# Gates, branch projections and merge of a hybrid decoder layer: features on the partitions against tokens on the partitions

## The chip, the core and the metric

The kernel runs on one core of a Trainium2 chip. The time is the device time of one execution in microseconds (us), the median of three. The core has five engines that this document names by the profile's short names: PE multiplies matrices (its weight loads are listed apart, as PEld), DVE and ACT work element by element on up to 128 partitions, POOL does the same more slowly, and SP issues the loads from HBM. Each engine takes its instructions in order and waits on semaphores that the others raise.

## The reference

One layer on 256 tokens of width 1024. The input, normalised, is multiplied by one wide matrix; its columns give the queries, keys, values and gates of two branches and two merge gates. Each branch ends in a gated activation of 256 x 1024, which has its own output projection. The change lies in the last lines:

```python
ret = jnp.einsum('bsv,vd->bsd', ret, w_ret_o)
mo = merge_heads(mo) * jax.nn.silu(mg)
mo = jnp.einsum('bsv,vd->bsd', mo, w_moba_o)
y = jax.nn.sigmoid(gr) * ret + jax.nn.sigmoid(gm) * mo
return x + jnp.einsum('bsd,de->bse', y, w_out)
```

A final RMSNorm follows.

## The kernel before, in words

All weights are streamed through the chip once, in 24 groups of 512 columns. A group comes as four chunks of two K tiles (a K tile is 128 of the 1024 rows). ACT rounds each chunk to a high part `wh` (L108) and DVE subtracts it from the raw chunk to get the low part `wl` (L109); both have eight buffers, so two groups fit. The loop splits group g + 1 and loads group g + 2 while PE multiplies group g. Products with at least 256 moving columns are made three times over, high by high, high by low and low by high, and accumulated in PSUM.

A group is multiplied in one of two layouts, both with the same 49,152 columns of PE work in a group:

- N, `proj_n` (L195 to L197): tokens on the partitions. The activations are the stationary operand, the weights move, 512 columns at a time. For each of two token tiles there are 8 K tiles of three products: 24 products.
- T, `proj_t` (L210, L211): features on the partitions. The weights are stationary, the activations move. For each of four feature tiles there are 8 K tiles of two products, one of 512 columns (high and low part of the activations side by side) and one of 256.

A unit is half a group: one token tile of N, or two feature tiles of T. Units run in order, u = 2 * group + half, and pieces of attention and small transposes are set ahead of some of them. The tile framework's scheduler orders each engine's instructions by the order of the code and the buffers that come free.

Groups 14 to 17 are the merge gates, 18 and 19 the retention branch's output projection, 20 and 21 that of the other branch, 22 and 23 the last projection. Before the change 14 to 21 are T, and the last projection is N. A T unit's PSUM is emptied for each feature tile in `evac_t`: ACT copies one half (L370), DVE adds the other (L371), and then comes a factor (L372): the token's 1/rms for gates, the gate itself for a branch. For groups 20 and 21 DVE adds the two branches (L407), ACT rounds the sum (L408) and DVE takes the low part (L409); that is `yT`, features on the partitions, which the last projection takes as its stationary operand as it is.

The retention branch's gated output is turned by PE in four sets of four 128 x 128 transposes (`ret_transpose`, L351) into a PSUM tile with one buffer, tag `t`. The last projection ends with the norm of each token tile and the stores.

Of the kernel before, what the change touches and what calls it, by code (L numbers as in the profile page):

```python
"""Hybrid decoder layer (RMSNorm, retention branch, MoBA branch, gated merge, residual, final RMSNorm)
for 256 tokens of width 1024 on one core.

Layouts: a tensor is "N" with tokens on the partitions and "T" with features on the partitions.
Each projection is either N (activations stationary, weights moving, 512 columns) or T (weights
stationary, activations moving, 256 tokens), so that the consumer finds the layout that it needs.

Products with at least 256 moving columns run in float32r (12-bit significands, one pass each): every
operand a is split exactly into a = ah + al with ah = round12(a), al = a - ah, and ah*bh + ah*bl + al*bh are
accumulated in float32. Attention products with 128 moving columns are plain float32 matmuls.  # L10

With 256 tokens the MoBA branch has a single block of 256, so no query has a past block: the top-k
selection is empty for any input, and each query attends causally to its own block.
"""
# [34 lines left out]
def hybrid_kernel(ctx: ExitStack, tc, xT, x, w_in, gn_w, w_ret_o, w_moba_o, w_out, fn_w, decay, out):  # L49
# [10 lines left out]
    def win(c):  # L60
# [8 lines left out]
        (win(GR), "T"), (win(GR + GW), "T"), (win(GM), "T"), (win(GM + GW), "T"),  # L69
        (w_ret_o[:, 0:GW], "T"), (w_ret_o[:, GW:], "T"),  # L70
        (w_moba_o[:, 0:GW], "T"), (w_moba_o[:, GW:], "T"),
# [19 lines left out]
    def cut(g, k):  # L91
        """Column ranges in which K tile k of group g is handled."""
        return (slice(0, S), slice(S, GW)) if (g, k) == (0, 0) else (slice(0, GW),)
# [24 lines left out]
    # K tile 0 of group 0 comes in two column ranges: its banks are started by products of zeros.  # L118
# [18 lines left out]
    # rel[q, k] = k - q for the causal pairs, MASKED for the others; query tile 0 with keys 0..127,  # L137
    # query tile 1 with keys 0..255.
# [16 lines left out]
    def rsqrt(y, a, tmp):  # L155
        """y = a ** -0.5 (a is kept): square root, exact reciprocal, one Newton step."""
        nc.scalar.activation(tmp, a, AF.Sqrt)
        nc.vector.reciprocal(y, tmp)
        nc.vector.tensor_mul(tmp, y, y)
        nc.vector.tensor_mul(tmp, tmp, a)  # L160
        nc.vector.tensor_scalar(tmp, tmp, -0.5, 1.5, op0=ALU.mult, op1=ALU.add)
        nc.vector.tensor_mul(y, y, tmp)
# [5 lines left out]
    def x_stats():  # L168
        """1 / rms per token: per partition for N, along the free axis for T."""
        ss = cst.tile([P, NT], F32, name="ss")  # L170
        tmp = cst.tile([P, NT], F32, name="sst")
        for t in range(NT):
            nc.scalar.activation(reto[:, t], xn[:, t], AF.Square, accum_out=ss[:, t:t + 1])
        nc.vector.tensor_scalar(ss, ss, 1.0 / D, EPS, op0=ALU.mult, op1=ALU.add)
        rsqrt(rs, ss, tmp)
# [10 lines left out]
    def proj_n(g, ah, al, t, c0=0, n=GW, ps=None):  # L186
        """[128 tokens of tile t, n columns of the group from c0], added to ps if that is given."""
        begun = ps is not None
        if not begun:
            ps = pm.tile([P, GW], F32, name="ps_m", tag="m")[:, :n]  # L190
        sl = slice(t * P, (t + 1) * P)
        for k in range(KT):
            for cs in cut(g, k) if g == 0 else (slice(0, n),):
                h, l = (w[g, k // 2][:, k % 2, c0 + cs.start:c0 + cs.stop] for w in (wh, wl))
                nc.tensor.matmul(ps[:, cs], ah[:, k, sl], h, start=not begun and k == 0, stop=False)  # L195
                nc.tensor.matmul(ps[:, cs], ah[:, k, sl], l, start=False, stop=False)  # L196
                nc.tensor.matmul(ps[:, cs], al[:, k, sl], h, start=False, stop=k == KT - 1)  # L197
        return ps

    def proj_t(g, a, i):  # L200
        """Feature tile i of the group: [128 features, 2, 256 tokens], the two halves still to be added.

        a(k) holds the high and the low part side by side, so that the high part of the weights meets both
        in one product of 512 columns.
        """
# [9 lines left out]
    qT, kT, V = {}, {}, {}  # L215
    # High and low parts of what the scores take in float32r: of the retention all queries and the first
    # 128 keys, of MoBA the last 128 queries and all keys.
# [126 lines left out]
    def ret_transpose(i):  # L344
        """Feature tiles 2i, 2i + 1 of the gated retention output, split."""
# [14 lines left out]
    G = {}  # L360
    mT = []
    yTh = yTl = None
    A = None

    def evac_t(g, i, ps):
        """Feature tile i of group g: adds the two halves of ps and applies what follows."""
        f = (i + 4) if g in (7, 8, 13, 15, 17, 19, 21) else i

        def scaled(out, w, eng=nc.gpsimd):
            nc.scalar.activation(out, ps[:, 1], AF.Copy)  # L370
            nc.vector.tensor_add(out, ps[:, 0], out)  # L371
            eng.tensor_mul(out, out, w)  # L372
# [22 lines left out]
        elif g in (14, 15, 16, 17):  # L395
            z = tmp("z")
            scaled(z, rsb)
            if i % 2 == 0:
                gt = new_v("gt")
                G[g // 16, f], G[g // 16, f + 1] = gt[:, :S], gt[:, S:]  # L400
            nc.scalar.activation(G[g // 16, f], z, AF.Sigmoid)  # L401
        elif g in (18, 19):
            scaled(A[:, f], G[0, f])
        elif g in (20, 21):
            z = tmp("z")
            scaled(z, G[1, f], nc.vector)
            nc.vector.tensor_add(z, z, A[:, f])  # L407
            nc.scalar.activation(yTh[:, f], z, AF.Copy)  # L408
            nc.vector.tensor_sub(yTl[:, f], z, yTh[:, f].bitcast(F32))  # L409

    def evac_n(g, t, ps):
# [17 lines left out]
        elif g in (10, 11):  # L429
            nc.scalar.activation(rgate[:, t, (g - 10) * GW:(g - 9) * GW], ps, AF.Copy, scale=r1)  # L430

# [8 lines left out]
    def unit(g, i):  # L440
        """Half i of group g: a token tile (N) or two feature tiles (T)."""
        nonlocal A, yTh, yTl, rgate
        if i == 0:
# [14 lines left out]
            if g == 18:  # L458
                A = ac.tile([P, KT, S], F32, name="A", tag="rgate")
            if g == 20:  # L460
                yT = ac.tile([P, 2, KT, S], F32R, name="yT", tag="xs")
                yTh, yTl = yT[:, 0], yT[:, 1]
        if groups[g][1] == "N":
            evac_n(g, i, proj_n(g, xh, xl, i, ps=ps0[i] if g == 0 else None))
        else:
            if g < 18:
                a = lambda k: xs[:, k]
            elif g < 20:
                a = lambda k: rT[k // 2][:, k % 2]
            else:  # L470
                a = lambda k: mT[k // 4][:, k % 4]
# [20 lines left out]
    # Unit u = 2 * group + half: the attention pieces come before the projection unit that they are set at.  # L492
# [15 lines left out]
    at(37, moba_split)  # L508

    nc.gpsimd.dma_start(gnw, gn_w)  # L510
    fnw = None
    for g in range(NG - 2):
        for i in range(2):
            u = 2 * g + i
            for c in (2 * i, 2 * i + 1):
                split(g + 1, c)
                if g + 2 < NG:
                    load(g + 2, c)
# [5 lines left out]
            if u == 38:  # L524
                # The last columns of x, split: TensorE adds them to the last product.
# [5 lines left out]
            if u == 40:  # L531
                fnw = ac.tile([P, D], F32, name="fnw", tag="qk", bufs=4)
                nc.sync.dma_start(fnw, fn_w.to_broadcast([P, D]))
                nc.gpsimd.tensor_scalar_mul(fnw, fnw, 2.0)
            for f, a in extra.get(u, []):
                f(*a)
            unit(g, i)
    for c in range(4):
        split(NG - 1, c)

    # Output projection, residual and final norm, one token tile after the other. Of the last columns
    # only what needs them is left for the end.
    r = ac.tile([P, NT, D], F32, name="r", tag="oT")
    sc = cst.tile([P, NT, 5], F32, name="sc")
    for t in range(NT):
        part, a, s, y, v = (sc[:, t, j:j + 1] for j in range(5))
        pieces = ((0, 512), (512, 1024)) if t == 0 else ((0, 512), (512, 768), (768, 1024))
        for j, (c0, c1) in enumerate(pieces):
# [4 lines left out]
            if c1 - c0 == S and last:  # L553
# [3 lines left out]
                proj_n(22 + c0 // GW, yTh, yTl, t, c0 % GW, c1 - c0, ps)  # L557
                nc.scalar.activation(sq, ps, AF.Square, accum_out=ss)
                nc.vector.tensor_mul(rr, ps, ww)
            else:  # L560
                ps = proj_n(22 + c0 // GW, yTh, yTl, t, c0 % GW, c1 - c0)
# [10 lines left out]
        # One Newton step from s, about sqrt(a): sqrt(a) = (s + a / s) / 2; the 2 is in fnw.  # L572
# [14 lines left out]
def _decay_table(np):  # L587
    """decay[m, h, :]: gamma_h ** (n - m) / sqrt(dk) for key m of tile 0 with queries n of 0..255, then for
    key m of tile 1 with the queries of tile 1; 0 where n < m."""
# [37 lines left out]
```

## Time and profile before

| | us |
|---|---|
| median of three runs (305.37 to 306.14) | 305.88 |
| span of the profiled execution, first to last instruction | 303.3 |
| PE busy in it | 294.0 |
| DVE, ACT, POOL busy in it | 219.7, 186.7, 79.0 |

The profile is of one execution; its span leaves out about 2.6 us around it. A matmul's row in the timeline has a start and a modelled end, and rows overlap, so what a product costs in a dense stretch is the distance from start to start.

### The profile page before, as it was taken

What the parts mean: (1) busy time and instruction counts of PE and PEld (TensorE: products, weight loads), DVE (VectorE), ACT (ScalarE), POOL (GpSimd) and SP (SyncE); (2) the same over time, 40 slices, a digit from 0 to 9 for tenths busy, and PEclk for the clock granted to TensorE, in tenths of its full rate; (3) what the DMA queues carried; (4) which work ended last, traced back from release to release, by engine and by line L of the source; (5) the groups of instructions that cost most, each with busy time, mean ns of one, the idle gap of its engine ahead of it and who ended that gap; (6) DMA issues with size and microseconds to landing.
All of it is one profiled execution on the core that took longest, in us unless ns stands there. A gap on an engine that the chain in (4) does not pass through costs nothing.

```text
span 303.3 us, 4584 instructions
## 1 busy us (share of the span) xinstructions
PE 294.0 (97%) x1628; PEld 253.9 (84%) x1628; DVE 219.7 (72%) x374; ACT 186.7 (62%) x358; POOL 79.0 (26%) x92
## 2 busy tenths in 40 slices
PE   8999989899999999999999999999999999999992
PEld 5778878799988899888888888888888888888891
DVE  3868676868699694884746799685784788899342
ACT  5786655755748676675966657476575556646231
POOL 3000185564520346300000132432432442300000
PEclk9999999999999999999999999999999999999998
DMA  7999967646384552746166264754835759540021
GB/s 188 361 405 407 319 166 244 212 161 193 91 254 108 189 181 100 195 143 218 36 240 200 79 163 123 216 166 168 261 93 201 253 177 304 169 140 0 0 73 69
DMA packets 28969, 55.11 MB, mean 182 GB/s; under 512 B 1937, under 2 KB 3985, under 8 KB 28945
## 3 DMA queue, kind: packets, MB, share of 16 engines
q1 hardware_dynamic: 28624, 54.54, 55.6%
q8 instruction: 13, 0.21, 0.3%
q10 hardware_dynamic: 288, 0.26, 0.3%
q14 instruction: 12, 0.09, 0.1%
q0 software_dynamic: 32, 0.00, 0.0%
HBM read 53.75 MB, written 1.05 MB: 181 GB/s over the span
## 4 chain that ended last, share of the span: by engine, by line
PE 89%; DVE 3%; POOL 3%; ACT 1%; issue 1%; DVEq 0%; ACTq 0%
PE ps_m L210 34%; PE ps_m L211 18%; PE ps_m L196 10%; PE ps_m L195 10%; PE ps_m L197 10%; DVE wl L109 2%; POOL qT L372 2%; POOL rqs L239 1%; PE ps_s L117 1%; PE ps_t L265 1%; ACT wh L108 1%; PE ps_s L244 1%; PE ps_o L284 1%; PE ps_t L351 1%; PE ps_o L316 1%
## 5 line engine op out<-in xcount | busy, mean ns | idle before, releaser
L210 PE MATMUL ps_m<-xs,wh 128*128 128x512 f32 x384 | 134.7, 393 | 0.0
L109 DVE TENSOR_TENSOR wl<-raw,wh 128x1024 fp32r<-128x1024 f32 x88 | 115.4, 1331 | 17.2 <-ACT wh L108 16.8
L211 PE MATMUL ps_m<-xs,wl 128*128 128x256 f32 x384 | 108.1, 282 | 1.1 <-DVE wl L109 1.1
L108 ACT ACTIVATE wh<-raw 128x1024 fp32r<-128x1024 f32 x88 | 90.1, 1052 | 4.4 <-PE ps_m L197 2.0
L210 PEld LDWEIGHTS ps_m<-xs,wh 128*128 128x128 f32 x384 | 72.1, 188 | 14.6
L211 PEld LDWEIGHTS ps_m<-xs,wl 128*128 128x128 f32 x384 | 72.7, 189 | 1.6 <-DVE wl L109 1.4
L372 POOL TENSOR_TENSOR z<-z,rsb 128x256 f32<-128x256 f32 x24 | 23.8, 990 | 88.4 <-DVE z L371 88.4
L196 PE MATMUL ps_m<-wl,xs 128*128 128x512 f32 (+1 forms) x98 | 38.9, 398 | 0.0
L197 PE MATMUL ps_m<-wh,xs 128*128 128x512 f32 (+1 forms) x98 | 38.8, 396 | 0.0
L195 PE MATMUL ps_m<-wh,xs 128*128 128x512 f32 (+1 forms) x98 | 38.7, 403 | 0.0
L196 PEld LDWEIGHTS ps_m<-wl,xs 128*128 128x128 f32 x98 | 19.0, 193 | 4.9 <-DVE wl L106 1.1
L195 PEld LDWEIGHTS ps_m<-wh,xs 128*128 128x128 f32 x98 | 18.9, 194 | 4.4 <-ACT wh L105 0.7
L197 PEld LDWEIGHTS ps_m<-wh,xs 128*128 128x128 f32 x98 | 18.9, 193 | 3.9
L210 PE MATMUL ps_m<-rT,wh 128*128 128x512 f32 x64 | 22.2, 390 | 0.0
L210 PE MATMUL ps_m<-mT,wh 128*128 128x512 f32 x64 | 22.2, 390 | 0.0
L371 DVE TENSOR_TENSOR z<-ps_m,z 128x256 f32<-128x256 f32 x32 | 13.4, 418 | 7.5 <-ACT z L370 7.5
L211 PE MATMUL ps_m<-rT,wl 128*128 128x256 f32 x64 | 18.1, 282 | 0.0
L211 PE MATMUL ps_m<-mT,wl 128*128 128x256 f32 x64 | 18.1, 282 | 0.0
L401 ACT ACTIVATE gt<-z 128x256 f32<-128x256 f32 x16 | 6.7, 418 | 16.8 <-POOL z L372 16.8
L210 PEld LDWEIGHTS ps_m<-rT,wh 128*128 128x128 f32 x64 | 12.0, 188 | 2.5
L210 PEld LDWEIGHTS ps_m<-mT,wh 128*128 128x128 f32 x64 | 12.0, 188 | 2.5
L195 PE MATMUL ps_m<-wh,yT 128*128 128x512 f32 (+1 forms) x40 | 14.0, 350 | 0.0
(171 smaller groups left out, 424.7 us busy)
## 6 DMA issues: line engine op xcount, KB each, us to landing
raw<-in_w_in SPq DMA_DIRECT2D x68, 512.0 KB, 4.7
raw<-in_w_ret_o SPq DMA_DIRECT2D x8, 512.0 KB, 5.1
raw<-in_w_moba_o SPq DMA_DIRECT2D x8, 512.0 KB, 5.0
raw<-in_w_out SPq DMA_DIRECT2D x8, 512.0 KB, 5.7
raw<-in_w_in SPq DMA_DIRECT2D x7, 256.0 KB, 4.5
xn<-in_x SPq DMA_DIRECT2D x2, 512.0 KB, 8.1
xt<-in_xT SPq DMA_DIRECT2D x7, 128.0 KB, 4.5
dec<-in_decay SPq DMA_DIRECT2D x1, 768.0 KB, 10.7
```

The lines of the kernel that those rows point to most:

```text
L108: nc.scalar.activation(h, r, AF.Copy)
L109: nc.vector.tensor_sub(l, r, h.bitcast(F32))
L117: nc.tensor.matmul(pw, warm[:, :P], warm, start=True, stop=True)
L195: nc.tensor.matmul(ps[:, cs], ah[:, k, sl], h, start=not begun and k == 0, stop=False)
L196: nc.tensor.matmul(ps[:, cs], ah[:, k, sl], l, start=False, stop=False)
L197: nc.tensor.matmul(ps[:, cs], al[:, k, sl], h, start=False, stop=k == KT - 1)
L210: nc.tensor.matmul(ps, h, a(k), start=k == 0, stop=False)
L211: nc.tensor.matmul(ps[:, 0], l, a(k)[:, 0], start=False, stop=k == KT - 1)
L239: nc.gpsimd.tensor_sub(out[:, 1], a, out[:, 0].bitcast(F32))
L371: nc.vector.tensor_add(out, ps[:, 0], out)
L372: eng.tensor_mul(out, out, w)
L401: nc.scalar.activation(G[g // 16, f], z, AF.Sigmoid)
```

## The change

Groups 14 to 21 become N. The merge gates are one ACT sigmoid of 128 x 512 straight from PSUM, with the token's 1/rms as a scale per partition. A branch's projection is multiplied by its gate on DVE, 128 x 512 at a time. The merged rows are then tokens on the partitions, but the last projection needs them with features there: `merge_transpose(t, c)` turns four 128 x 128 tiles on PE into one PSUM tile of tag `t`, ACT rounds it to the high part of `yT` and DVE takes the low part. It is called four times. The units of groups 20 and 21 now run 20.0, 21.0, 20.1, 21.1, so that token tile 0 is complete two units before token tile 1, and the splits of groups 22 and 23 move with them. The split of the other branch's output (`moba_split`) and the residual's last columns (`xr`) are set two units earlier.

```diff
-        (win(GR), "T"), (win(GR + GW), "T"), (win(GM), "T"), (win(GM + GW), "T"),
-        (w_ret_o[:, 0:GW], "T"), (w_ret_o[:, GW:], "T"),
-        (w_moba_o[:, 0:GW], "T"), (w_moba_o[:, GW:], "T"),
+        (win(GR), "N"), (win(GR + GW), "N"), (win(GM), "N"), (win(GM + GW), "N"),
+        (w_ret_o[:, 0:GW], "N"), (w_ret_o[:, GW:], "N"),
+        (w_moba_o[:, 0:GW], "N"), (w_moba_o[:, GW:], "N"),
...
-        elif g in (14, 15, 16, 17):
-            z = tmp("z")
-            scaled(z, rsb)
-            if i % 2 == 0:
-                gt = new_v("gt")
-                G[g // 16, f], G[g // 16, f + 1] = gt[:, :S], gt[:, S:]
-            nc.scalar.activation(G[g // 16, f], z, AF.Sigmoid)
-        elif g in (18, 19):
-            scaled(A[:, f], G[0, f])
-        elif g in (20, 21):
-            z = tmp("z")
-            scaled(z, G[1, f], nc.vector)
-            nc.vector.tensor_add(z, z, A[:, f])
-            nc.scalar.activation(yTh[:, f], z, AF.Copy)
-            nc.vector.tensor_sub(yTl[:, f], z, yTh[:, f].bitcast(F32))
...
+        elif g in (14, 15, 16, 17):
+            G[g // 16, t, g % 2] = gt = new_v("gt")
+            nc.scalar.activation(gt, ps, AF.Sigmoid, scale=r1)
+        elif g in (18, 19):
+            nc.vector.tensor_mul(A[:, t, (g - 18) * GW:(g - 17) * GW], ps, G[0, t, g % 2])
+        elif g in (20, 21):
+            z, y = G[1, t, g % 2], A[:, t, (g - 20) * GW:(g - 19) * GW]
+            nc.vector.tensor_mul(z, ps, z)
+            nc.vector.tensor_add(y, y, z)
+
+    def merge_transpose(t, c):
+
+        ps = pa.tile([P, 4, P], F32, name="ps_t", tag="t", bufs=1)
+        for j in range(4):
+            k = 4 * c + j
+            nc.tensor.transpose(ps[:, j], A[:, t, k * P:(k + 1) * P], ident)
+        h, l = (yT[:, 4 * c:4 * c + 4, j, t * P:(t + 1) * P] for j in range(2))
+        nc.scalar.activation(h, ps, AF.Copy)
+        nc.vector.tensor_sub(l, ps, h.bitcast(F32))
...
-    for g in range(NG - 2):
+    for g in range(NG - 4):
...
+    for i in range(2):
+        stream(20, i)
+    yT = ac.tile([P, KT, 2, S], F32R, name="yT", tag="xs")
+    unit(20, 0)
+    unit(21, 0)
+    unit(20, 1)
+    for c in range(2):
+        merge_transpose(0, c)
+    for i in range(2):
+        stream(21, i)
+    unit(21, 1)
...
+            if t == 0:
+                merge_transpose(1, j)
```

The order of the built program shows where the scheduler puts the new pieces. On PE, before, the last product of group 21 (`mT` is the other branch's output, `ps_m` a projection's PSUM) is followed at once by the last projection:

```order
L210 MATMUL ps_m<-mT_2568,wh 128x512
L211 MATMUL ps_m<-mT_2568,wl 128x256
L195 MATMUL ps_m<-wh,yT 128x512
L196 MATMUL ps_m<-wl,yT 128x512
L197 MATMUL ps_m<-wh,yT 128x512
```

On PE, of the change, the same place: the last product of unit 20.1, the first set of merge transposes and the start of unit 21.1; then the second set, after 16 of the 24 products of 21.1; then the first product of the last projection. (The names of tokens' merged rows are `A`, of the transposes' PSUM `ps_t`.)

```order
L197 MATMUL ps_m<-wh,mT_2332 128x512
L431 MATMUL ps_t<-ident,A 128x128 x4
L195 MATMUL ps_m<-wh,mT_2331 128x512
...
L195 MATMUL ps_m<-wh,mT_2332 128x512
L431 MATMUL ps_t<-ident,A 128x128 x4
L196 MATMUL ps_m<-wl,mT_2332 128x512
...
L195 MATMUL ps_m<-wh,yT 128x512
```

The sets are split apart: the second stands not behind the first but inside the next unit.

On DVE, of the change, the merge of token tile 0 (L423, L424 twice), the splits of group 22 (L109), the product of unit 20.1, the last split of group 22, its sum, and the low part of the first set (L434), which has to be done before the second set may overwrite `ps_t`:

```order
L423 TENSOR_TENSOR gt<-ps_m,gt 128x512
L424 TENSOR_TENSOR A<-A,gt 128x512
L109 TENSOR_TENSOR wl<-raw,wh 128x1024 x3
L423 TENSOR_TENSOR gt<-ps_m,gt 128x512
L109 TENSOR_TENSOR wl<-raw,wh 128x1024
L424 TENSOR_TENSOR A<-A,gt 128x512
L434 TENSOR_TENSOR yT<-ps_t,yT 128x4x128
L106 TENSOR_TENSOR wl<-raw,wh 128x512 x3
L434 TENSOR_TENSOR yT<-ps_t,yT 128x4x128
```

A whole split and a sum stand between the product of 20.1 and the first low part.

On ACT, of the change, there: the splits of groups 20, 21 and 22 in a row, and then the high parts of the sets (L433) between those of group 23 (L105):

```order
L108 ACTIVATE wh<-raw 128x1024 x12
L433 ACTIVATE yT<-ps_t 128x4x128
L105 ACTIVATE wh<-raw 128x512 x4
L433 ACTIVATE yT<-ps_t 128x4x128
```

The first high part stands behind the last split of group 22.

## Rows read from the trace of the kernel before

**Rows 1.** The page: span, busy time, slices, chain that ended last.

```profile
span 303.3 us, 4584 instructions
...
PE 294.0 (97%) x1628; PEld 253.9 (84%) x1628; DVE 219.7 (72%) x374; ACT 186.7 (62%) x358; POOL 79.0 (26%) x92
...
PE   8999989899999999999999999999999999999992
...
POOL 3000185564520346300000132432432442300000
PEclk9999999999999999999999999999999999999998
...
PE 89%; DVE 3%; POOL 3%; ACT 1%; issue 1%; DVEq 0%; ACTq 0%
```

**Rows 2.** What PE waited for in the span: total, times, longest.

```profile
PE ps_s L117 <- DVE warm L114: 1.2, 1, 1.2
PE ps_o L316 <- DVE il L303: 1.1, 1, 1.1
PE ps_m L211 <- DVE wl L109: 1.1, 1, 1.1
```

**Rows 3.** PE in four stretches: length, busy (instructions), clock, DMA share, GB/s.

```profile
122.25:127.85 5.60, 5.60 (x27) 1.00 0.76 200
213.42:274.53 61.11, 61.11 (x355) 1.00 0.59 196
274.53:291.33 16.80, 16.80 (x75) 1.00 0.02 8
178.42:189.97 11.55, 11.55 (x70) 1.00 0.54 147
```

**Rows 4.** Timeline of PE around transposes: start us, length us, instruction, count.

```profile
189.85 0.28 PE L211 MATMUL ps_m<-xs,wl 128*128 128x256 f32 x1
189.97 0.60 PE L351 MATMUL ps_t<-ident,reto 128*128 128x128 f32 x4
190.33 0.48 PE L210 MATMUL ps_m<-xs,wh 128*128 128x512 f32 x1
```

**Rows 5.** Groups of PE instructions: busy us, mean ns, idle before.

```profile
L351 PE MATMUL ps_t<-ident,reto 128*128 128x128 f32 x16 | 2.4, 273 | 0.0
```

**Rows 6.** Groups of POOL, ACT and DVE that the change removes in part.

```profile
L372 POOL TENSOR_TENSOR z<-z,rsb 128x256 f32<-128x256 f32 x24 | 23.8, 990 | 88.4 <-DVE z L371 88.4
...
L401 ACT ACTIVATE gt<-z 128x256 f32<-128x256 f32 x16 | 6.7, 418 | 16.8 <-POOL z L372 16.8
...
L371 DVE TENSOR_TENSOR z<-ps_m,z 128x256 f32<-128x256 f32 x32 | 13.4, 418 | 7.5 <-ACT z L370 7.5
```

**Rows 7.** Groups of ACT and DVE: splits, and 128x512 from PSUM.

```profile
L108 ACT ACTIVATE wh<-raw 128x1024 fp32r<-128x1024 f32 x88 | 90.1, 1052 | 4.4 <-PE ps_m L197 2.0 <-DMA raw<-in_w_in 1.5 <-PE ps_m L210 0.6
...
L430 ACT ACTIVATE rgate<-ps_m,rs 128x512 f32<-128x512 f32 x4 | 2.7, 682 | 6.3 <-PE ps_m L197 6.2
...
L109 DVE TENSOR_TENSOR wl<-raw,wh 128x1024 fp32r<-128x1024 f32 x88 | 115.4, 1331 | 17.2 <-ACT wh L108 16.8 <-PE ps_o L283 0.2
...
L562 DVE TENSOR_TENSOR r<-ps_m,xn 128x512 f32<-128x512 f32 x3 | 2.1, 692 | 4.5 <-PE ps_m L197 4.5
```

**Rows 8.** Timeline of DVE: two single splits.

```profile
193.45 1.76 DVE L109 TENSOR_TENSOR wl<-raw,wh 128x1024 fp32r<-128x1024 f32 x1
...
266.08 1.22 DVE L109 TENSOR_TENSOR wl<-raw,wh 128x1024 fp32r<-128x1024 f32 x1
```

**Rows 9.** Timeline of all engines at the end.

```profile
296.65 0.28 PE L196 MATMUL ps_m<-wl,yT 128*128 128x256 f32 x1
...
296.76 0.28 PE L197 MATMUL ps_m<-wh,yT 128*128 128x256 f32 x1
...
297.12 0.28 PE L197 MATMUL ps_m<-wh,yT 128*128 128x256 f32 x1
297.49 0.38 ACT L558 ACTIVATE sq<-ps_m 128x256 f32<-128x256 f32 x1 [2.15 <-PE ps_m L197]
```

More of the change, by code (lines that the diff above doesn't have):

```diff
@@ L183, in x_stats_t, with proj_n @@
         nc.scalar.activation(rsq, ps[:, :S], AF.Copy, scale=1.0 / math.sqrt(P))
-    def proj_n(g, ah, al, t, c0=0, n=GW, ps=None):
+    def proj_n(g, a, t, c0=0, n=GW, ps=None):
         begun = ps is not None
@@ L194, in proj_n @@
                 h, l = (w[g, k // 2][:, k % 2, c0 + cs.start:c0 + cs.stop] for w in (wh, wl))
-                nc.tensor.matmul(ps[:, cs], ah[:, k, sl], h, start=not begun and k == 0, stop=False)
-                nc.tensor.matmul(ps[:, cs], ah[:, k, sl], l, start=False, stop=False)
-                nc.tensor.matmul(ps[:, cs], al[:, k, sl], h, start=False, stop=k == KT - 1)
+                nc.tensor.matmul(ps[:, cs], a(k)[:, 0, sl], h, start=not begun and k == 0, stop=False)
+                nc.tensor.matmul(ps[:, cs], a(k)[:, 0, sl], l, start=False, stop=False)
+                nc.tensor.matmul(ps[:, cs], a(k)[:, 1, sl], h, start=False, stop=k == KT - 1)
         return ps
@@ L361, in hybrid_kernel, with scaled @@
     mT = []
-    yTh = yTl = None
+    yT = None
     A = None
     def evac_t(g, i, ps):
-        f = (i + 4) if g in (7, 8, 13, 15, 17, 19, 21) else i
-        def scaled(out, w, eng=nc.gpsimd):
+        f = (i + 4) if g in (7, 8, 13) else i
+        def scaled(out, w):
             nc.scalar.activation(out, ps[:, 1], AF.Copy)
             nc.vector.tensor_add(out, ps[:, 0], out)
-            eng.tensor_mul(out, out, w)
+            nc.gpsimd.tensor_mul(out, out, w)
         def tmp(n):
@@ L440, in unit @@
     def unit(g, i):
-        nonlocal A, yTh, yTl, rgate
+        nonlocal A, yT, rgate
         if i == 0:
@@ L458, in unit @@
             if g == 18:
[L459 to L462, printed above, removed]
+                A = ac.tile([P, NT, D], F32, name="A", tag="rgate")
+        if g < 18:
+            a = lambda k: xs[:, k]
+        elif g < 20:
+            a = lambda k: rT[k // 2][:, k % 2]
+        else:
+            a = lambda k: mT[k // 4][:, k % 4]
         if groups[g][1] == "N":
-            evac_n(g, i, proj_n(g, xh, xl, i, ps=ps0[i] if g == 0 else None))
+            evac_n(g, i, proj_n(g, a, i, ps=ps0[i] if g == 0 else None))
         else:
[L466 to L471, printed above, removed]
             for f in (2 * i, 2 * i + 1):
@@ L507, in hybrid_kernel, with stream @@
         at(27 + 2 * i, ret_transpose, i)
-    at(37, moba_split)
+    at(35, moba_split)
     nc.gpsimd.dma_start(gnw, gn_w)
-    fnw = None
-    for g in range(NG - 2):
+    def stream(g, i):
+        for c in (2 * i, 2 * i + 1):
+            split(g + 1, c)
+            if g + 2 < NG:
+                load(g + 2, c)
+    for g in range(NG - 4):
         for i in range(2):
             u = 2 * g + i
[L515 to L518, printed above, removed]
+            stream(g, i)
             if u == 0:
@@ L523, in hybrid_kernel @@
                 x_stats_t()
-            if u == 38:
+            if u == 36:
                 xr = new_v("xr", F32R)
@@ L530, in hybrid_kernel @@
                 nc.vector.tensor_sub(xr[:, S:], xn[:, 1, D - S:], xr[:, :S].bitcast(F32))
[L531 to L534, printed above, removed]
             for f, a in extra.get(u, []):
@@ L537, in hybrid_kernel, with ya @@
             unit(g, i)
+    fnw = ac.tile([P, D], F32, name="fnw", tag="qk", bufs=4)
+    nc.sync.dma_start(fnw, fn_w.to_broadcast([P, D]))
+    nc.gpsimd.tensor_scalar_mul(fnw, fnw, 2.0)
+    for i in range(2):
[9 more added lines that the diff above has]
+    unit(21, 1)
     for c in range(4):
         split(NG - 1, c)
+    def ya(k):
+        return yT[:, k]
     r = ac.tile([P, NT, D], F32, name="r", tag="oT")
@@ L556, in hybrid_kernel @@
                 nc.tensor.matmul(ps, ir, xr[:, S:], start=False, stop=False)
-                proj_n(22 + c0 // GW, yTh, yTl, t, c0 % GW, c1 - c0, ps)
+                proj_n(22 + c0 // GW, ya, t, c0 % GW, c1 - c0, ps)
                 nc.scalar.activation(sq, ps, AF.Square, accum_out=ss)
@@ L560, in hybrid_kernel @@
             else:
-                ps = proj_n(22 + c0 // GW, yTh, yTl, t, c0 % GW, c1 - c0)
+                ps = proj_n(22 + c0 // GW, ya, t, c0 % GW, c1 - c0)
                 nc.vector.tensor_add(rr, ps, xn[:, t, c0:c1])
```

## The prediction

> **What bounds the kernel now.** The page comes first: PE is busy for 294.0 of 303.3 us, its slices read 8 or 9 but for the last, its granted clock reads 9 throughout, the upper of its two levels (2.4 GHz); the chain that ended last is PE for 89% [rows 1]. Busy time of PE is made of overlapping rows, so the second view is PE's own waits: three in the whole span, 3.4 us together [rows 2]. The first is the start, the other two wait for DVE at 43.7 and 60.3 us, long before the change begins (its first unit, 28, stands one unit before the transposes at 189.97, near 184 us). So from 60 us on PE waits for nothing, and a change behind that point is worth what it adds to or takes from PE's own instructions, plus any wait that it makes. Work taken from DVE, ACT and POOL earns nothing.
>
> The third view is therefore PE's length for a unit. Eleven T units from 213.42 to 274.53 take 61.11 us, 5.555 each; all of them belong to groups that change. The first three N units of the last projection take 16.80, 5.600 each, and a lone N unit among attention pieces takes 5.60 as well [rows 3]. The fourth is what four transposes cost between projection products: they start at 189.97 and the next product at 190.33 [rows 4].
>
> **The change part by part.** *T to N.* Eight groups are 16 units. Each goes from 5.555 to 5.600: 16 x 0.045 = +0.7 us. From below: if an N product ran at T's time per column, the unit would be 5.555 too and the term 0. From above: without the one slow resumption after transposes (0.08) in the window, T is 5.548, and the term 0.8. I take 0.7, since the N row is the very form that is added.
>
> A rule on this stands in the Trainium skill, "TensorE: Matmul & The Clock Gate", section "Back-to-back issue gap": each matmul costs its columns plus a fixed 2.5 ns, so fewer and longer ones should win. By its figures, as an estimate, the 24 products of N would take 5.18 us and the 32 of T 5.20, and the term would be -0.3 instead of +0.7. The trace does not agree: both units are longer than that, and N is the longer one [rows 3]. The sum goes by the rows.
>
> *Transposes.* There are 16 more, in four sets of four, of the kind and number of the retention's sets, again between float32r products. The stretch from one set to the next holds a set and two T units: 11.55 - 2 x 5.555 = 0.44 us for a set [rows 3], 0.36 of it the set itself [rows 4] and the rest, 0.08, a slower first product behind it. Four sets: +1.8 us. From below 0.36 a set, 1.4; from above one after the other at 273 ns each, 16 x 0.273 = 4.4 [rows 5]. I take 1.8, the row that is the same operation in the same place. Before, the merge needed none of this, since `yT` came out of the sum in the right layout, beside PE.
>
> *What goes off the other engines.* POOL loses 16 of the 24 multiplies of the z row (0.99 us each) and eight of A, ACT 16 sigmoids of 0.42, 32 copies and eight roundings, DVE 32 adds of 0.42, 24 of them in the z row, and 24 operations of the merge [rows 6]; in their place stand eight sigmoids and four roundings on ACT and 16 operations on DVE, of 128 x 512 and some 0.7 us [rows 7]. All of it lay beside PE, which had no wait there, so I cost it at nothing. The freed time has no taker either.
>
> *Weights.* An N group asks for its chunks over its first 5.6 us, a T group for all four inside its first feature tile; and N frees each chunk's buffer in its second unit, in order. Both are easier than before. The exception is groups 20 and 21: group 21 is needed one unit earlier, but its last buffer comes free at the end of unit 19.1, a whole unit (5.6 us) ahead, against 1.05 on ACT and 1.33 on DVE for a split [rows 7]. Group 22 is freed chunk by chunk in unit 20.1 and needed a unit later. SP's order of loads is the same. I cost this at nothing; without that cover one split is 2.4 us.
>
> *The new wait.* The PSUM tile of the transposes has one buffer. The second set must wait for the low part of the first, and the DVE order puts a product, a split and a sum ahead of that. Set the start of the first set to 0. PE is ready for the second at 0.44 + 16 x 0.2333 = 4.17. The last product of 20.1 ends at 0.17; ACT then splits the last chunk of group 22 to 1.25 (1.05) and rounds the set to 1.93 (0.68); DVE has done its product by 0.9, waits for ACT, splits from 1.25 to 2.58 (1.33), sums to 3.27 and takes the low part to 3.96 (0.69 each) [rows 7]. That leaves 0.2 less the hand-overs. At 1.22 for the split there is no wait, at 1.76 (both stand in the trace) it is about 0.3 [rows 8]. I take 0.1. Behind that wait on PE stand eight products of unit 21.1 and the whole last projection, so it counts in full. From above: nothing covered, which is the third rival. The two sets of token tile 1 each have a whole unit of 5.6 us between them and their readers, and cost no wait.
>
> *The end.* The last product starts at 297.12, and ACT takes up its result at 297.49 [rows 9]; from there to the end of the span at 303.3 the instructions are the same, so the end moves with PE.
>
> Sum: 0.7 + 1.8 + 0.1 = +2.6 us. The profiled span becomes 305.9. Its execution had 303.3 where the median of the runs is 305.88, 2.6 us outside the span, which stay. The time is 308.5.
>
> **The rivals.** *The early waits go.* The two waits for DVE, 1.1 each [rows 2], could fall out of the schedule when the code behind them is smaller: 308.5 - 2.2 = 306.3. Against it: DVE's and PE's instructions up to there stand in the same order, and what made DVE late is not touched.
>
> *N is faster in these places, and the change gains.* The mechanism: T's spacing was held up by what DVE and POOL do beside it, and with that work gone the products close up. Two rows of 256 columns start 0.11 apart [rows 9]; two such for 512 columns would be a unit of 24 x 0.22 = 5.28, and 16 x (5.28 - 5.555) + 1.9 = -2.5, so 303.4. It decides from a unit of 5.555 - 1.9/16 = 5.44 down. Against it: the three units of the last projection had POOL idle [rows 1] and took 5.600, to the hundredth what the unit beside attention took [rows 3].
>
> *The sets are not covered.* If DVE or ACT comes to the high or low part late, PE stands still with the set. A set wholly uncovered costs 0.68 + 0.69 [rows 7], and with the split and the sum ahead of it 2.0 more; half of that on the first token tile gives 1.7 in place of the 0.1, so 310.1. For it: the cover is only 0.2 us. Against it: each further delay has to come from one of four instructions of known length.
>
> *Transposes one after the other.* 16 x 0.273 = 4.4 [rows 5] instead of 1.8 gives 311.1. Against it: four of them started and were passed in 0.36 [rows 4]. The Trainium skill, same page, section "Part 4: PE-mode transpose", gives about 275 ns for one in a kernel; as a duration the trace agrees with 273, but the starts lie 0.09 apart, and by the page's figure taken as a price this rival's time would come out.
>
> **How the numbers follow.** Forecast 0.80; early waits gone 0.06; N faster 0.03; sets not covered 0.09; transposes one after the other 0.02. A measurement of this kernel tells 0.3%, 0.9 us, from no change. The forecast and the last two are slower by more, 0.91; the early waits give 0.4 us, no change, 0.06; faster 0.03. The range for 8 in 10 goes from 307.5 (T to N at 0, sets at 0.36, no wait: +1.4, with a little for the spread of the runs, 0.4) halfway into the uncovered sets, 309.9.
>
> **What would show it.** In the profile after: N units at 5.60 from the merge gates on; 0.44 from the start of a merge set to where the next product would have been; PE's waits still three, with at most a short one at the second merge set for DVE's low part; the span from last product to end 6 us as before; POOL idle from the silu gates on but for the norm weights. It is wrong if N units differ from 5.60, if a PE wait of over half a microsecond stands behind 184 us, or if either early wait is gone.

## The result and the profile after

The changed kernel takes 308.38 us, median of four runs (307.83 to 308.59), beside 305.81 for the kernel before (305.37 to 306.14, four runs). The ratio is 1.0083, with an interval of 1.0069 to 1.0097: 2.6 us slower, as forecast (308.5). One of the six executions of a kernel below, the one with the transposes alone, ran at a granted clock of 0.56 and took 493.47 us; its numbers are of the other five.

The page of the changed kernel answers to [rows 1]: span, busy time of each engine, slices of PE, POOL and the clock, chain that ended last.

```profile
span 306.8 us, 4230 instructions
...
PE 296.6 (97%) x1516; PEld 248.0 (81%) x1516; DVE 205.6 (67%) x334; ACT 177.3 (58%) x314; POOL 56.8 (19%) x68
...
PE   8999989899999999999999999999999999999992
...
POOL 3000086564520345300000222100000003000000
PEclk9999999999999999999999999999999999999999
...
PE 84%; DMA 4%; DVE 4%; POOL 3%; ACT 2%; SPq 1%; issue 1%; DVEq 0%; ACTq 0%
```

There are 354 instructions fewer, POOL's busy time falls by 22 us, DVE's by 14 and ACT's by 9, and the kernel is slower. PE executes 112 instructions fewer too and is busy for 2.6 us more. The clock reads 9 in every slice, its upper level; before, the last slice reads 8. POOL is idle behind the silu gates but for one slice, the norm weights.

PE's own waits answer to [rows 2] (total, times, longest):

```profile
PE ps_s L117 <- DVE warm L114: 1.2, 1, 1.2
PE ps_o L316 <- DVE il L303: 1.1, 1, 1.1
PE ps_m L211 <- DVE wl L109: 1.1, 1, 1.1
PE ps_m L196 <- DVE wl L109: 0.5, 1, 0.5
PE ps_m L195 <- ACT wh L105: 0.4, 2, 0.2
```

The first three are those of before, the two early ones for DVE included. The last two stand between 6.84 and 18.65 us, in the loads of the first weights, where the two kernels have the same code. Behind the last of them the kernel after is 0.94 us late (the next `L197` product starts at 18.99, before at 18.05), and the first transposes still are: the set that is at 178.42 before [rows 3] is at 179.35 after. (That the waits add up to 0.9 too is chance: ahead of the last one the kernel after was only 0.13 late, as the kernel before had started its first products of 256 columns 0.21 apart until 6.8 us and the one after 0.12 apart from 5.5 us on.) So 0.9 of the 3.5 us between the two spans is not the change. In the kernels below, waits in these loads come to between nothing and 1.6 us, and three that have them (0.2, 0.2 and 0.7) are the kernel before with an edit behind that point.

The comparison that is free of it starts at the first product behind that set and ends at the modelled end of PE's last product. First the kernel before, then the one after (length, busy and instructions, clock, DMA share, GB/s):

```profile
178.78:297.40 118.62, 118.62 (x681) 1.00 0.48 156
```

```profile
179.70:300.88 121.18, 121.18 (x569) 1.00 0.48 152
```

PE is busy throughout in both, and the difference is 2.56 us: the change, in PE's own instructions. It has the parts that the sum named. An N unit beside attention, ten N units in a row, and the stretch from the first merge set to the second:

```profile
185.35:190.94 5.59, 5.59 (x26) 1.00 0.31 84
214.57:270.65 56.08, 56.08 (x243) 1.00 0.54 171
270.65:274.83 4.18, 4.18 (x22) 1.00 0.67 234
```

The ten units begin behind a set of transposes, whose slow first product (0.08) is in the window: (56.08 - 0.08) / 10 = 5.600, the value of the last projection's units in [rows 3].

The timeline of PE around the first two merge sets (start us, length us, instruction, count) answers to [rows 4]:

```profile
270.65 0.60 PE L431 MATMUL ps_t<-ident,A 128*128 128x128 f32 x4
271.01 0.48 PE L195 MATMUL ps_m<-wh,mT 128*128 128x512 f32 x1
271.32 0.40 PE L196 MATMUL ps_m<-wl,mT 128*128 128x512 f32 x1
...
274.83 0.61 PE L431 MATMUL ps_t<-ident,A 128*128 128x128 f32 x4
275.19 0.48 PE L196 MATMUL ps_m<-wl,mT 128*128 128x512 f32 x1
```

A set is 0.36 us to the next product, and that product is 0.31 from its successor where 0.23 is usual: 0.44 in all. The second set begins 4.18 us behind the first, and 4.17 was what PE's own instructions ask for. So PE lost nothing there, but its cover was thin. This is DVE there, the last row being the low part of the first set, and then the weight load of the second set:

```profile
270.56 1.23 DVE L109 TENSOR_TENSOR wl<-raw,wh 128x1024 fp32r<-128x1024 f32 x1 [0.18 <-ACT wh L108]
271.70 0.68 DVE L423 TENSOR_TENSOR gt<-ps_m,gt 128x512 f32<-128x512 f32 x1
272.30 1.22 DVE L109 TENSOR_TENSOR wl<-raw,wh 128x1024 fp32r<-128x1024 f32 x1
273.43 0.69 DVE L424 TENSOR_TENSOR A<-A,gt 128x512 f32<-128x512 f32 x1
274.03 0.69 DVE L434 TENSOR_TENSOR yT<-ps_t,yT 128x512 fp32r<-128x512 f32 x1
```

```profile
274.77 0.42 PEld L431 LDWEIGHTS ps_t<-ident,A 128*128 128x128 f32 x4 [0.22 <-DVE yT L434]
```

The low part ends at 274.72, 0.11 us before the set. Hardly any of that is to spare: the set's weight load stood idle for 0.22 until the low part was done and began 0.05 behind its end. On PE the set starts 0.24 behind the product before it (274.59), where 0.23 is usual.

The four instructions that the prediction lined up follow in its order, but later: a split of an earlier chunk (first row) holds DVE until 271.79, so the product of 20.1 ends at 272.38, 1.73 behind the start of the first set where the prediction had 0.9. The last split then starts 0.4 late (272.30), and split, sum and low part take 2.42 instead of 2.71: the split took the shorter of its two values (1.22), and rows that follow each other on DVE overlap by 0.09.

### The profile page after: what moved, and what is told of

It reads as the page before. It is cut to its first block, busy times and chain, and to the rows that moved or that the text cites. A ratio compares the mean times of both kernels' runs of the same rounds, so it can differ in the third digit from the quotient of the medians.

```text
span 306.8 us, 4230 instructions
## 1 busy us (share of the span) xinstructions
PE 296.6 (97%) x1516; PEld 248.0 (81%) x1516; DVE 205.6 (67%) x334; ACT 177.3 (58%) x314; POOL 56.8 (19%) x68
## 4 chain that ended last, share of the span: by engine, by line
PE 84%; DMA 4%; DVE 4%; POOL 3%; ACT 2%; SPq 1%; issue 1%; DVEq 0%; ACTq 0%
PE ps_m L196 18%; PE ps_m L197 18%; PE ps_m L195 18%; PE ps_m L210 14%; PE ps_m L211 8%; DVE wl L109 2%; DMA raw<-in_w_in 2%; DMA xt<-in_xT 2%; POOL qT L372 2%; ACT wh L108 1%; POOL rqs L239 1%; PE ps_t L265 1%; SPq L87 1%; PE ps_s L244 1%; PE ps_o L284 1%
## 5 line engine op out<-in xcount | busy, mean ns | idle before, releaser
L109 DVE TENSOR_TENSOR wl<-raw,wh 128x1024 fp32r<-128x1024 f32 x88 | 112.2, 1290 | 28.0 <-ACT wh L108 27.6
L210 PE MATMUL ps_m<-xs,wh 128*128 128x512 f32 x256 | 89.9, 393 | 0.0
L211 PE MATMUL ps_m<-xs,wl 128*128 128x256 f32 x256 | 72.0, 282 | 1.1 <-DVE wl L109 1.1
L196 PE MATMUL ps_m<-wl,xs 128*128 128x512 f32 (+1 forms) x162 | 64.0, 396 | 0.5 <-DVE wl L109 0.5
L195 PE MATMUL ps_m<-wh,xs 128*128 128x512 f32 (+1 forms) x162 | 64.0, 400 | 0.4 <-ACT wh L105 0.4
L197 PE MATMUL ps_m<-wh,xs 128*128 128x512 f32 (+1 forms) x162 | 63.9, 394 | 0.0
L210 PEld LDWEIGHTS ps_m<-xs,wh 128*128 128x128 f32 x256 | 48.0, 188 | 9.7
L211 PEld LDWEIGHTS ps_m<-xs,wl 128*128 128x128 f32 x256 | 48.4, 189 | 1.6 <-DVE wl L109 1.4
L195 PEld LDWEIGHTS ps_m<-wh,xs 128*128 128x128 f32 x162 | 30.6, 190 | 8.1 <-ACT wh L105 1.4
L197 PEld LDWEIGHTS ps_m<-wh,xs 128*128 128x128 f32 x162 | 30.6, 189 | 6.8
L372 POOL TENSOR_TENSOR z<-z,rsb 128x256 f32<-128x256 f32 x8 | 8.2, 1024 | 57.6 <-DVE z L371 57.6
L195 PE MATMUL ps_m<-wh,yT 128*128 128x512 f32 (+1 forms) x40 | 14.2, 354 | 0.0
L197 PE MATMUL ps_m<-wh,yT 128*128 128x512 f32 (+1 forms) x40 | 14.0, 350 | 0.0
L197 PE MATMUL ps_m<-wh,rT 128*128 128x512 f32 x32 | 12.7, 396 | 0.0
L195 PE MATMUL ps_m<-wh,rT 128*128 128x512 f32 x32 | 12.7, 396 | 0.0
```

The lines of the kernel that those rows point to most:

```text
L109: nc.vector.tensor_sub(l, r, h.bitcast(F32))
L195: nc.tensor.matmul(ps[:, cs], a(k)[:, 0, sl], h, start=not begun and k == 0, stop=False)
L196: nc.tensor.matmul(ps[:, cs], a(k)[:, 0, sl], l, start=False, stop=False)
L197: nc.tensor.matmul(ps[:, cs], a(k)[:, 1, sl], h, start=False, stop=k == KT - 1)
L210: nc.tensor.matmul(ps, h, a(k), start=k == 0, stop=False)
L211: nc.tensor.matmul(ps[:, 0], l, a(k)[:, 0], start=False, stop=k == KT - 1)
```

## The experiments

Each kernel was timed beside the kernel before on the same chip. The ratio is to that kernel. "PE's stretch" is measured as above, from the first product behind the set of transposes near 179 us to the end of the last product: 118.62 before, 121.18 after.

**The transposes taken out of the change.** The changed kernel, with `merge_transpose` reading the merged rows as they stand; the transposes of the merge are left out, so the last projection multiplies untransposed rows.

```diff
-        ps = pa.tile([P, 4, P], F32, name="ps_t", tag="t", bufs=1)
-        for j in range(4):
-            k = 4 * c + j
-            nc.tensor.transpose(ps[:, j], A[:, t, k * P:(k + 1) * P], ident)
+        ps = A[:, t, c * GW:(c + 1) * GW].rearrange("p (a b) -> p a b", b=P)
```

> The changed kernel without the 16 merge transposes on PE: ACT and DVE make the parts of yT straight from the merged rows, so the last projection multiplies untransposed rows (that part of the computation is left out). Theory of the sum (PE is the bound, transposes cost 0.44 a set): the four sets go, 308.4 - 1.8 = 306.6, that is +0.7 to +0.8 over the kernel before (ratio 1.0025), and from the start of unit 28 to the last product 112.97 + 0.7 = 113.7 us. Rival (the loss sits in the new order of units and its waits, the transposes lie beside something): 308.0 to 308.4, ratio 1.007 or more.

Ratio 1.002 (1.001 to 1.003). PE's stretch:

```profile
180.70:300.12 119.42, 119.41 (x553) 1.00 0.49 154
```

That is 0.80 above before: T to N alone, 16 x 0.05. The medians, 306.51 and 305.82, say 0.7, and 306.6 was expected.

**The transposes alone.** The kernel before, with four sets of four transposes of `xn` at units 36, 38, 40 and 42, whose results nobody reads.

```diff
+    def idle_set():
+        ps = pa.tile([P, 4, P], F32, name="ps_t", tag="t", bufs=1)
+        for j in range(4):
+            nc.tensor.transpose(ps[:, j], xn[:, 0, j * P:(j + 1) * P], ident)
...
+    for u in (36, 38, 40, 42):
+        at(u, idle_set)
```

> The kernel before, with four sets of four 128x128 float32 transposes of a resident tile ahead of units 36, 38, 40 and 42, whose result nobody reads. Theory of the sum: 4 x 0.44 = +1.8 us, 307.6, ratio 1.0058, and PE's stretch from unit 28 to the last product 112.97 + 1.76 = 114.7. Rival (transposes cost their full duration one after the other, 273 ns): +4.4 or more, 310.2. Rival (they hide): 305.8.

Ratio 1.005 (1.0036 to 1.0063). PE's stretch:

```profile
179.16:299.59 120.43, 120.43 (x697) 1.00 0.48 153
```

It is 1.81 above before, 0.45 a set. With the 0.80 of the first experiment that makes 2.61, beside the 2.56 of the whole change. Nothing is left over for a wait. The medians are coarser: 307.30 and 305.82 say 1.5 here, and 1.5 + 0.7 = 2.2 beside 2.6; the interval of this ratio alone reaches from 1.1 to 1.9 us.

**A second bank for the second set.** If the single buffer made the second set wait, another buffer takes that wait away.

```diff
-        ps = pa.tile([P, 4, P], F32, name="ps_t", tag="t", bufs=1)
+        ps = pa.tile([P, 4, P], F32, name="ps_t" if c == 0 else "ps_o", tag="t" if c == 0 else "o", bufs=1)
```

> The changed kernel with the second set of each token tile in another PSUM bank, so that it need not wait for the low part of the first; the scheduler then puts both sets of token tile 0 side by side. Theory of the sum: the wait was worth 0 to 0.1 us, and one of the slow first products behind a set (0.08) may go, so 308.2 to 308.4, no difference. Rival (the single PSUM buffer costs something that the wait view does not show): under 308.0.

Ratio 1.0075 (1.0059 to 1.0092). The two sets now stand side by side:

```profile
270.38 0.60 PE L431 MATMUL ps_t<-ident,A 128*128 128x128 f32 x4
270.81 0.60 PE L431 MATMUL ps_o<-ident,A 128*128 128x128 f32 x4
271.17 0.48 PE L195 MATMUL ps_m<-wh,mT 128*128 128x512 f32 x1
```

Eight transposes take 0.79, with the slow product behind them 0.87, where two sets apart take 2 x 0.44 = 0.88: the one slow product that is saved (0.08) is lost again between the sets, which start 0.43 apart instead of 0.36. PE's stretch is 0.03 below the changed kernel:

```profile
179.43:300.58 121.15, 121.15 (x569) 1.00 0.48 152
```

The wait was worth nothing that can be told. The median, 308.04 (307.72 to 308.79), is 0.2 below what was expected and just above the 308.0 under which the rival would have been right; the runs of the two kernels overlap, and the stretch decides.

**The cover taken away.** The rival with sets that are not covered needs a version in which it is true: the first token tile's sets are called behind unit 21.1 instead of ahead of it, so that their readers, the last projection's products, follow directly.

```diff
-    for c in range(2):
-        merge_transpose(0, c)
     for i in range(2):
         stream(21, i)
     unit(21, 1)
+    for c in range(2):
+        merge_transpose(0, c)
```

> The changed kernel with both sets of token tile 0 set behind unit 21.1, right ahead of the last projection, so nothing covers the first set's way through ACT. Theory of the sum: PE stands still for about ACT's 0.6 us and the hand-overs behind the first set, and somewhat for DVE's 0.7 us low part: +1.0 to +1.4, 309.4 to 309.8, with PE waits for ACT L433 or DVE L434 that the changed kernel has not. Rival (PE has other work there or the path is short anyway): within 0.3 us of the changed kernel, 308.4.

Ratio 1.0127 (1.0106 to 1.0149), the medians 1.4 us above the changed kernel. Two waits appear that are in none of the other kernels (PE's waits, then its timeline):

```profile
PE ps_m L195 <- ACT yT L433: 0.8, 1, 0.8
PE ps_t L431 <- DVE yT L434: 0.2, 1, 0.2
```

```profile
275.88 0.60 PE L431 MATMUL ps_t<-ident,A 128*128 128x128 f32 x4
277.24 0.50 PE L195 MATMUL ps_m<-wh,yT 128*128 128x512 f32 x1 [0.77 <-ACT yT L433]
...
278.62 0.66 PE L431 MATMUL ps_t<-ident,A 128*128 128x128 f32 x4 [0.19 <-DVE yT L434]
```

From the first set to the next product are 1.36 us instead of 0.36. A wait of 0.77 in the view of waits is 1.0 from start to start, since the view counts from the modelled end of the row before; the 0.19 is 0.35 in the same way (the product ahead starts at 278.04). PE's stretch is 1.40 above the changed kernel:

```profile
179.32:301.90 122.58, 121.62 (x569) 1.00 0.47 150
```

So the rival's mechanism exists and has the price that was expected; with one projection unit ahead of the readers it is covered in the changed kernel.

**Why an N unit is longer.** The columns are equal in T and N (2 x 24 x 512 = 24,576 in a group, half of the figure given with the two layouts above), so the form of the products must make the 0.05. In the changed kernel, groups 14 to 17 are computed in other forms, compared unit by unit in one profile: other orders of the three products (14, 15), halves of 256 columns, 46 products instead of 24 (16), and both token tiles taking turns in two banks (17).

```diff
...
+                if g == 16:
+                    for m, (x, y) in enumerate(((ah, h), (ah, l), (al, h))):
+                        halves = (slice(0, GW),) if k == m == 0 or (k, m) == (KT - 1, 2) else (slice(0, S), slice(S, GW))
+                        for cj in halves:
+                            nc.tensor.matmul(ps[:, cj], x, y[:, cj], start=k == m == 0, stop=(k, m) == (KT - 1, 2))
...
+                three = ((ah, h), (al, h), (ah, l)) if g == 14 else ((ah, l), (ah, h), (al, h))
...
+                            nc.tensor.matmul(two[t], a(k)[:, j, t * P:(t + 1) * P], y,
```

> The changed kernel with the four gate groups in four forms of the N product, all of the same columns: group 14 in the order high-high, low-high, high-low; group 15 with the weights' low part first; group 16 with two products of 256 columns in place of nearly each of 512; group 17 with the two token tiles taking turns, so that neighbouring products accumulate in different PSUM banks. The profile's length of each unit tells what makes N 5.600 where T is 5.555. If the order of operands or the reuse of a stationary matters, group 14 or 15 differs from 5.60; if two products in a row on one bank matter, group 17 is shorter, 5.55 or less a unit; if a product has a cost of its own, group 16 is longer by 46 times that: at 2.5 ns 5.66 or so for half the extra products, 5.72 at 5 ns. If none of them, all are 5.60 and the 0.045 stays unexplained.

A unit of group 14, a unit of group 15, a unit of group 16, and both units of group 17:

```profile
184.35:189.95 5.60, 5.60 (x26) 1.00 0.32 91
195.99:201.59 5.60, 5.60 (x26) 1.00 0.71 234
207.62:213.29 5.67, 5.67 (x47) 1.00 0.86 251
219.40:230.60 11.20, 11.20 (x50) 1.00 0.84 263
```

The kernel's time is one run (307.72 beside 305.5) and is not used; the units are. Neither the order nor the bank moves the unit from 5.60. Twenty-two more products cost 0.07, 3 ns each. So each product has a small price of its own, and by that T, with 32 products, should be longer than N with 24. It is shorter. The Trainium skill, "TensorE: Matmul & The Clock Gate", section "Back-to-back issue gap", has such a price, 2.5 ns on top of its columns, given there for a single matmul by itself. On the halves the trace agrees with it in size; T's shorter unit goes against it. What makes T short was not in these forms.

**T's own form.** In the kernel before, group 14 computes a feature tile as eight products of 512 columns and then eight of 256, instead of the two kinds taking turns. Group 15 (its branch is left out here) cuts 12 of a unit's 16 products of 512 in two, so that a unit has 44 products, most of them of 256.

```diff
...
+            if g == 14:
+                for k in range(KT):
+                    nc.tensor.matmul(ps, part(wh, k), a(k), start=k == 0, stop=False)
+                for k in range(KT):
+                    nc.tensor.matmul(ps[:, 0], part(wl, k), a(k)[:, 0], start=False, stop=k == KT - 1)
...
```

> The kernel before, with two groups of gates in other forms of the T product, same columns. Group 14: for each feature tile first the eight products of 512 columns, then the eight of 256. Group 15: nearly every product of 512 as two of 256, so 24 of the 32 products of a unit become 36 more or less in a row of 256. It asks why a T unit takes 5.555 where an N unit of as many columns takes 5.600. If a T product is cheaper by itself (its moving operand, its bank), group 14 stays at 5.555 and its 512s start 0.2305 apart. If only the turn from 512 to 256 columns is cheap, the 512s in a row start 0.2333 apart as in N and the unit grows to 5.60. Group 15 grows by its extra products times the cost of a product, 3.2 ns each by the run on the N forms (some 12 in a unit from 32 to 44, +0.04).

Again one run (305.91 beside 304.73), read by its units. The timeline of group 14's first unit:

```profile
184.96 2.02 PE L214 MATMUL ps_m<-xs,wh 128*128 128x512 f32 x8
186.83 1.09 PE L216 MATMUL ps_m<-xs,wl 128*128 128x256 f32 x8
187.76 2.03 PE L214 MATMUL ps_m<-xs,wh 128*128 128x512 f32 x8
189.63 1.10 PE L216 MATMUL ps_m<-xs,wl 128*128 128x256 f32 x8
190.57 0.60 PE L371 MATMUL ps_t<-ident,reto 128*128 128x128 f32 x4
```

The unit, 184.96 to 190.57, is 5.61: the same products of the same layout, in another order, have lost T's advantage. In a row the 512s start (186.83 - 184.96) / 8 = 0.234 apart, as N's do, and the 256s 0.116; a pair is 0.350. Taking turns, a pair is 5.555 / 16 = 0.347. So the 0.05 of a unit comes from long and short products in turns, and not from which operand is stationary. Why turns are 3 ns cheaper stays open.

The first unit of group 15:

```profile
196.61:202.26 5.65, 5.65 (x46) 1.00 0.43 110
```

It is 0.10 above a T unit, where 0.04 was expected for its 12 more products. Above the unit in rows, 5.61, it is 0.04, 3 ns each, which fits a form that has lost the turns as well and pays for the cuts on top.

**The early waits.** The first rival would have taken the two waits for DVE away. What it would be worth is tested on the kernel before, where a multiply by the token's 1/rms in groups 2 and 3 goes from POOL to DVE, eight instructions.

```diff
-            scaled(a, rsb)
+            scaled(a, rsb, nc.vector)
```

> The kernel before, with the factor of the retention's queries and keys (groups 2 and 3) multiplied on DVE (0.42 us) in place of POOL (0.74 to 1.7), so that ACT's splits do not stand behind POOL. Theory (PE is the bound, its waits and its instructions are all that counts): the two waits of PE for DVE, 1.1 us each and 1.3 with the hand-over, get shorter or go, and the time falls by what they lose, up to 2.5 us, 303.3. Rival (DVE has no room for eight more multiplies there, and the splits come as late as before): the same two waits, 305.8.

Ratio 0.9909 (0.9888 to 0.9929): 302.65 us beside 305.5, 2.85 less where up to 2.5 was expected. PE's waits are now these:

```profile
PE ps_s L117 <- DVE warm L114: 1.2, 1, 1.2
PE ps_m L195 <- ACT wh L105: 0.7, 1, 0.7
```

Both waits for DVE are gone. The stretch from the first unit of group 2 to the first of group 6, before and then with the edit:

```profile
28.99:82.89 53.90, 51.69 (x313) 1.00 0.65 204
```

```profile
29.55:80.64 51.09, 51.09 (x313) 1.00 0.68 214
```

It is 2.81 shorter, 2.21 of that the two waits. The other 0.60 stands in the rows of the same two places. In the kernel before, the two products that waited on PE and rows of ACT, POOL and DVE ahead of them are these:

```profile
40.63 0.42 ACT L238 ACTIVATE rqs<-qT 128x256 fp32r<-128x256 f32 x1 [1.73 <-POOL qT L372]
...
43.69 0.39 PE L211 MATMUL ps_m<-xs,wl 128*128 128x256 f32 x1 [1.10 <-DVE wl L109]
...
58.20 1.63 POOL L372 TENSOR_TENSOR kT<-kT,rsb 128x256 f32<-128x256 f32 x1 [2.03 <-DVE kT L371]
...
59.17 1.08 DVE L303 TENSOR_TENSOR il<-inn,ih 128x384 fp32r<-128x384 f32 x1
...
60.30 0.39 PE L316 MATMUL ps_o<-vh,il 128*128 128x256 f32 x1 [1.11 <-DVE il L303]
```

The products ahead start at 42.20 and 58.92, so from start to start each wait costs 1.26 (1.49 where 0.23 is usual, 1.38 where 0.12 is). The products that waited start their successors 0.10 and 0.11 late, and the product at 58.72 its own 0.08 late. The sum is 2.81.

DVE has eight instructions more and holds PE up less. At the first wait ACT had stood 1.73 us for POOL's multiply, its split came late, and DVE's split, on which PE waits, stood idle 1.70 for that. At the second, POOL's multiply stood beside DVE's late work: 1.63 us for the one at 58.20, and DVE's subtract `il` took 1.08 beside it (0.54 with the edit). On DVE the multiply takes 0.55 and 0.48 on average (queries, keys). The Trainium skill, "SBUF — State Buffer", section "SBUF: two separate sides", says that DVE with two SBUF inputs and POOL take turns on one port pair, the later one blocked. The rows fit it, but this run changes POOL's load and DVE's order together and does not separate them. This version beats both kernels, and joining it with the change was not tried.

## Why the prediction was right

*What bounds the kernel.* PE, with no wait behind 60 us. It held: taking 45 us of busy time off POOL, DVE and ACT gave nothing, and the change cost what it added to PE.

*T to N, +0.7.* Measured 0.80, the upper bound that the prediction gave: T without the slow product in its window. The 0.7 was thus 0.1 short.

*Transposes, +1.8.* Measured 1.81 alone, and 0.44 a set in the changed kernel. The lower price, 0.36 a set, leaves out the slow product behind each; the price of one after the other, 273 ns, is a duration, and the four start 0.09 apart.

*The wait of the second set, +0.1.* Mis-sized: nothing on PE. The way there was not the one lined up either. DVE was not free for the product by 0.9 but held by an earlier split until 1.14 behind the set's start, which the prediction left out though the order of DVE shown ahead of it has three splits before that product; the rest was shorter than lined up. The single splits behind 193 us, beside an idle POOL, took 1.21 to 1.23, and the mean of 1.33 that was put in stood for splits with POOL busy as well (1.76 [rows 8]; in the changed kernel the one at 253.80, beside POOL's norm weights, took 2.09). That the low part came just in time is luck: the set's weight load was already waiting for it. This 0.1 too much and the 0.1 too little of T to N cancel in the sum of 2.6.

*What goes off the other engines, and the weights, at nothing.* Held. Behind 19 us PE waits for no split or load that it did not wait for before.

*The 2.6 us outside the span.* This step was wrong, though it did not hurt. It took the difference between the profiled span and the median of other runs as time outside the span. Runs with both numbers show 1.7 to 1.9: 308.59 and 306.8 for the changed kernel, 305.05 and 303.3 for one execution of the kernel before. A span of 303.3 is thus an execution some 0.8 below the median. The forecast of the time stands on the difference, and that went to the median; the forecast of the span, 305.9, missed by 0.9, the waits in the loads. The ends of the range do not follow from their terms: +1.4 is 307.3 and halfway to the uncovered sets is 309.3, where 307.5 and 309.9 stand, and 0.4 for the spread brings neither. The measured time lies inside all of them.

*The rivals.* The early waits stayed, 1.1 each; worth 2.8 when they go, where the rival said 2.2, and the change did not touch them. N came no faster in any place, and its price was misread: the 0.11 between two rows of 256 columns was one pair, and over 24 of them in the kernel before (291.33 to 294.17) it is 0.118. Two of those are 0.237, a unit of 5.68, longer and not shorter; the unit in halves measured 5.67. Uncovered sets cost 1.4 over the changed kernel when made so, where the rival said 1.6 (1.7 in place of 0.1). Transposes one after the other did not happen.

## What to carry to other kernels

Where PE has no waits, a change is worth the difference of PE's start-to-start distances, however many instructions leave the other engines; take them from rows of the same form in the same kernel, and add what the first instruction behind the new ones loses. A layout that needs transposes pays for them on the engine that is the bound, even when they hide no wait. And compare two profiles from a point where the code is still the same, else the scatter of the start is read as the change.

## What the runs showed of the hardware

- Long and short products in turns (512 and 256 columns) are 0.347 us a pair, each kind in a row 0.350 (the kernel before; group 14 in T's own form). A unit of 16 pairs gains 0.05 us; over 16 units that is a third of this change.
- Cutting products in two costs 3 ns for each one more (0.07 for 22 in a unit of N, 0.04 for 12 in one of T beside the unit in rows). In the last projection products of 256 columns start 0.118 apart, though the row of each one's weight load is 188 ns long.
- The first float32r product behind a set of float32 transposes starts its successor 0.08 us late (0.31 to 0.32 behind it instead of 0.23), at each of the sets of four in the changed kernel.
- The loads of the first weights scatter: PE waits between nothing and 1.6 us in them, in kernels with the same code there.
